# Hybrid decoder trunk: activations stationary, 512 weight columns streaming, in gates, branch products, GLU, w_out and down projection

## The chip, the cores and the metric

The kernel runs on one core of a Trainium2 chip. The metric is the device time of one execution in microseconds (us); the runs below give it for the kernel before. A profile is one execution taken by the hardware profiler; its span runs from the first to the last instruction. TensorE multiplies (PE in the rows, PEld its weight loads), VectorE is DVE, ScalarE ACT, GpSimd POOL, SyncE SP.

## The reference

One layer for 256 tokens of 2048 features, in float32:

```python
hn = rmsnorm(h, norm_mix_w)
proj = hn @ w_in          # u, q, k, v, r, a_lr, dq, dk, dv and the 3 x 2048 gates
y_a = s5_branch(u, ...)   # state space, gelu, @ w_glu, val * sigmoid(gate)
y_b = gla_branch(...)     # linear attention, 4 heads, norm * silu(r), @ gla_w_br
y_c = diff_attn_branch(...)          # 4 heads, norm, @ diff_w_br
g = sigmoid(gates)
merged = g[0] * y_a + g[1] * y_b + g[2] * y_c
h = h + merged @ w_out
h = h + conv_gated_mlp(rmsnorm(h, norm_ffn_w), w_up, conv_w, conv_b, w_down)
out = rmsnorm(h, norm_final_w)
```

## The kernel before

All weights come as 4504 blocks of 128x128 in the order of use, eight blocks (a half chunk, 512 KB) per load. `load` issues the load on SP's queue; `split` rounds it on ScalarE to fp32r (`wh`) and takes the remainder on VectorE (`wl`), three half chunks ahead of their use. Activations are kept the same way, as slots of 512 columns: 256 tokens of the high part, then 256 of the low part, features on the partitions (`hlx`, `hlm`, `hlz`). A product with a weight is high x high + low x high + high x low.

`run` emits the matmuls of a job (one output tile). In kind "a" the weight block is stationary and the activations stream, so that outputs have features on the partitions: a bank of 512 columns holds high and low sums side by side, and `full` adds the two halves (a ScalarE copy, a VectorE add). In kind "b", used for v and dv, the activations are stationary and two weight blocks stream, for each of two token halves; two banks are held and nothing is left to add:

```python
self.mm(bank, wh[:, c:c + P], x, st, False, True)                   # "a", 512 columns
self.mm(bank[:, 0:T], wl[:, c:c + P], x[:, 0:T], False, en, True)   # "a", 256 columns
self.mm(bank, xh, wh[:, c:c + 2 * P], st, False, True)              # "b", 256 columns each
self.mm(bank, xl, wh[:, c:c + 2 * P], False, False, True)
self.mm(bank, xh, wl[:, c:c + 2 * P], False, en, True)
```

The order is written out by hand. After each half chunk `tick` steps every open generator once: evictions (`evs`), attention (`bgs`), and the S5 branch (`s5`) as far as an estimate of VectorE's and ScalarE's load allows. A generator of the last jobs of a stage (`hot`) is urgent: a tick steps it up to 40 times, so that all its instructions are emitted at once. `need` inserts ticks until an input is marked done. Every engine's queue runs in order of emission.

Stages in order: u (8 tiles), the low-rank gate, linear attention (k, q, v, r for 4 heads), differential attention (dq, dk, dv), 16 tiles each of gate B with its branch product and gate C with its own, 7 tiles of gate A (`NA`), GLU with the other gates (S5's result in `hlz` must be done), w_out, FFN up (43 value and 43 gate tiles) and down in two parts. From the end of u until S5 is done three of the eight PSUM banks serve these jobs; the others belong to S5 and the attention heads. The sums of squares of the two later norms (`add_ss`) are squares on ScalarE, adds on GpSimd and a product with a matrix of ones.

Of the kernel before, what the change touches and what calls it, by code (L numbers as in the profile page):

```python
# [34 lines left out]
H_LR = NU * KD // HB  # L35

# [16 lines left out]
class Slots:  # L53
    def __init__(self, aps, slow=False):
        self.aps, self.slow, self.late = aps, slow, []
        self.free = list(range(len(aps)))
        self.back = {}

    def take(self, n):
        if len(self.free) < n:  # L60
            return None
        got, self.free = self.free[:n], self.free[n:]
        return got


def grab(pool, n=1):
    while True:
        got = pool.take(n)
        if got is not None:
            return [(pool, i, pool.aps[i]) for i in got]  # L70
        yield None
# [14 lines left out]
def give(pool, *slots):  # L86
    for _, _, ap in slots:
        pool.free.append(len(pool.aps))
        pool.aps.append(ap)


class Builder:
    SLACK = 1300

    def __init__(self, ctx, tc, wpk, xT, cst, smask, wg, dtab, bpk, cpk, cup, dpk, out):
        self.tc, self.nc = tc, tc.nc
        self.wpk, self.xT, self.cst_d = wpk, xT, cst
# [27 lines left out]
        self.pool = Slots([ar[:, S_END + i * T:S_END + (i + 1) * T] for i in range(N_POOL)])  # L125
        o = S_END + N_POOL * T
        self.evp = Slots([ar[:, o + i * T:o + (i + 1) * T] for i in range(N_EVP)])
        o += N_EVP * T
        self.rp = Slots([ar[:, o + i * T:o + (i + 1) * T] for i in range(N_RES)])
# [192 lines left out]
    def pair(self, a, b, cut):  # L322
        n = len(a[0])
        self.run([a[:2] + ("a", a[2]), b[:2] + ("a", b[2])],
                 [(t, i) for r in (range(cut), range(cut, n)) for t in range(2) for i in r])

    def run(self, tiles, order, hot=()):
        ps = [None] * len(tiles)
        seen = set()
        for t, i in order:  # L330
            xs, evac, kind, keys = tiles[t]
            nb = len(xs)
            per = 2 if kind == "b" else 1
            if ps[t] is None:
                n = 0
                while len(self.g.free) < per:
# [5 lines left out]
                ps[t] = [(self.g, e, self.g.aps[e]) for e in self.g.take(per)]  # L342
# [518 lines left out]
    def ev_v(self, name, h):  # L861
        def gen(ps):
            for t in range(2):
                (s,) = yield from grab(self.pool)
                self.act(s[2], ps[t][2][:, 0:T], AF.Copy)
# [99 lines left out]
    def head_out(self, ob, h, nw, base, rname):  # L965
# [6 lines left out]
        for i in range(2):  # L972
            self.act(S[i][2], ob[2][:, i * T:(i + 1) * T], AF.Square, accum_out=q[:, 20 + i:21 + i])
        if rname:
            for d in range(2):
                yield from self.wait((rname, h, d))
            rr = [self.proj[rname, h, d] for d in range(2)]
            for d in range(2):
                self.act(rr[d][2], rr[d][2], AF.Silu)
        yield from self.rstd(q[:, 20:22], 1.0 / T, q[:, 22:24], self.tiny[:, 0:2], True)  # L980
        for i in range(2):
            self.act(S[i][2], ob[2][:, i * T:(i + 1) * T], AF.Copy, scale=q[:, 22 + i:23 + i])
        drop(ob)
        yield None
# [8 lines left out]
        if rname:  # L993
            for d in range(2):
                self.stt(S[d][2], src[d], nw[:, d:d + 1], rr[d][2], ALU.mult, ALU.mult)
            drop(b, *rr)
            yield None
            for d in range(2):
                self.hilo(dst[d], S[d][2])
            yield None  # L1000
            for d in range(2):
                self.lopart(dst[d], S[d][2])
        else:
            for d in range(2):
                self.hilo(dst[d], src[d], scale=nw[:, d:d + 1])
            yield None
            for d in range(2):
                self.lopart(dst[d], src[d], scale=nw[:, d:d + 1])
            drop(b)
# [5 lines left out]
    def diff_body(self):  # L1015
# [68 lines left out]
        give(self.pool, dt, *S)  # L1084

# [1 line left out]
    def ev_sig(self, name, j, pool):  # L1087
        def gen(ps):
            s = yield from self.full(ps[0])
            yield None  # L1090
            (o,) = yield from grab(pool)
            self.act(o[2], s[2], AF.Sigmoid)
            drop(s)
            self.proj[name, j] = o
            self.done.add((name, j))
        return gen

    def ev_yb(self, j):
        def gen(ps):
            s = yield from self.full(ps[0])  # L1100
            yield from self.wait(("sB", j))
            g = self.proj["sB", j]
            self.tt(g[2], s[2], g[2], ALU.mult)
            drop(s)
            self.proj["m", j] = g
# [385 lines left out]
```

## Time and profile before

| | us |
|---|---|
| device time, median of 3 runs | 1699.87 (1692.81 to 1701.56) |
| the profiled execution, span | 1698.8 |
| TensorE busy in it | 1671.6 (98%) |
| VectorE, ScalarE, GpSimd busy | 1156.9, 975.8, 149.8 |
| granted TensorE clock, mean | 0.992 |

The profiled execution's own time is known as its span; it lies 1.1 us below the median. Busy time of TensorE is a union of listed durations, which overlap their successors: how fast it works is read from the distance between starts.

### The profile page before, as it was taken

The numbers are of one execution on the slowest core, as the hardware profiler recorded it, in microseconds if no ns is written. First come the engines' busy times: TensorE is split into PE (matmuls) and PEld (weight loads), VectorE is DVE, ScalarE is ACT, GpSimd is POOL, SyncE is SP. The second block draws the span as 40 slices with busy tenths as digits, with TensorE's granted clock in tenths as the row PEclk, the third lists the DMA queues.
The fourth block names the chain that finished last, engine by engine and source line by source line (L and its number), as shares of the span: only waits on it lengthen the run. The fifth ranks groups of instructions, "written<-read, shape, count | busy, mean of one in ns | idle before, by whom it ended". The sixth has DMA issues, their size and how long they took to land.

```text
span 1698.8 us, 27107 instructions
## 1 busy us (share of the span) xinstructions
PE 1671.6 (98%) x10352; PEld 1459.3 (86%) x10352; DVE 1156.9 (68%) x1923; ACT 975.8 (57%) x1570; POOL 149.8 (9%) x153
## 2 busy tenths in 40 slices
PE   8899999999999999999999999999999999999996
PEld 7688889999888888888888888888888888888885
DVE  7877667667877677566656777777644677777544
ACT  6557766666566566555555655555544455555553
POOL 1500000000000111000014200000011000000222
PEclk9899999999999999999999999999999999999998
DMA  7567454554656656665555555555555555555552
GB/s 258 167 192 183 144 167 159 167 160 156 211 176 206 204 177 200 199 236 186 186 186 187 186 186 186 186 186 186 186 187 186 185 187 187 186 187 184 189 185 98
DMA packets 111298, 312.97 MB, mean 184 GB/s; under 512 B 27840, under 2 KB 38464, under 8 KB 111040
## 3 DMA queue, kind: packets, MB, share of 16 engines
q1 hardware_dynamic: 109760, 309.54, 56.6%
q8 instruction: 81, 1.33, 0.3%
q10 hardware_dynamic: 1216, 1.18, 0.2%
q0 software_dynamic: 192, 0.52, 0.1%
q14 instruction: 49, 0.40, 0.1%
HBM read 304.64 MB, written 4.19 MB: 182 GB/s over the span
## 4 chain that ended last, share of the span: by engine, by line
PE 96%; DVE 2%; ACT 1%; DMA 1%; issue 0%; DVEq 0%; SPq 0%; ACTq 0%
PE bank L150 95%; PE bank L154 1%; DVE hlx L171 1%; DVE wl L164 0%; DVE ar L164 0%; DMA ar<-in_xT_dram 0%; DMA raw<-in_wpk_dram 0%; ACT ar L158 0%; ACT wh L158 0%; ACT L158 0%; DVEq L1486 0%; ACT hlm L158 0%; DVE ar L171 0%; DVE wh L164 0%; SPq L387 0%
## 5 line engine op out<-in xcount | busy, mean ns | idle before, releaser
L164 DVE TENSOR_TENSOR wl<-raw,wh 128x1024 fp32r<-128x1024 f32 (+1 forms) x564 | 692.0, 1229 | 490.1 <-ACT wh L158 487.1
L150 PE MATMUL bank<-hlx,wh 128*128 128x512 f32 x2656 | 947.6, 398 | 0.0
L158 ACT ACTIVATE wh<-raw 128x1024 fp32r<-128x1024 f32 (+1 forms) x564 | 594.3, 1056 | 604.9 <-issue 319.5
L150 PE MATMUL bank<-hlx,wl 128*128 128x256 f32 x2656 | 748.5, 282 | 0.0
L150 PEld LDWEIGHTS bank<-hlx,wh 128*128 128x128 f32 x2656 | 499.1, 188 | 122.4 <-issue 3.8
L150 PEld LDWEIGHTS bank<-hlx,wl 128*128 128x128 f32 x2656 | 498.9, 188 | 0.2
L150 PE MATMUL bank<-hlm,wh 128*128 128x512 f32 x1152 | 413.3, 398 | 2.6 <-ACT wh L158 2.6
L150 PE MATMUL bank<-hlm,wl 128*128 128x256 f32 x1152 | 326.4, 283 | 1.0 <-DVE wl L164 1.0
L150 PEld LDWEIGHTS bank<-hlm,wh 128*128 128x128 f32 x1152 | 217.9, 189 | 55.7 <-ACT wh L158 3.5
L167 POOL TENSOR_TENSOR ar<-ar 128x256 f32<-128x256 f32 (+2 forms) x127 | 141.8, 1128 | 1218.2 <-ACT ar L158 744.3
L150 PEld LDWEIGHTS bank<-hlm,wl 128*128 128x128 f32 x1152 | 217.8, 189 | 2.0 <-DVE wl L164 1.9
L158 ACT ACTIVATE ar<-bank 128x256 f32<-128x256 f32 (+4 forms) x424 | 152.4, 380 | 28.5 <-PE bank L150 26.7
L150 PE MATMUL bank<-hlz,wh 128*128 128x512 f32 x432 | 154.4, 396 | 0.0
L164 DVE TENSOR_TENSOR ar<-ar 128x256 f32<-128x256 f32 (+5 forms) x360 | 139.6, 392 | 9.2 <-ACT ar L158 1.5
L164 DVE TENSOR_TENSOR ar<-bank,ar 128x256 f32<-128x256 f32 x286 | 118.8, 417 | 12.0 <-ACT ar L158 9.3
L150 PE MATMUL bank<-hlz,wl 128*128 128x256 f32 x432 | 121.8, 282 | 0.0
L158 ACT ACTIVATE ar<-ar 128x256 f32<-128x256 f32 (+3 forms) x209 | 83.9, 413 | 25.6 <-DVE ar L164 21.3
L150 PEld LDWEIGHTS bank<-hlz,wh 128*128 128x128 f32 x432 | 81.2, 188 | 19.6
L150 PE MATMUL bank<-wh,hlx 128*128 128x256 f32 x512 | 90.8, 281 | 0.0
L171 DVE SCALAR_TENSOR_TENSOR ar<-ar,cst 128x256 f32<-128x256 f32 x173 | 83.3, 482 | 5.7 <-ACT ar L158 2.7
L150 PEld LDWEIGHTS bank<-hlz,wl 128*128 128x128 f32 x432 | 81.1, 188 | 0.0
L150 PEld LDWEIGHTS bank<-wh,hlx 128*128 128x128 f32 x512 | 77.7, 188 | 1.9 <-issue 1.4
(81 smaller groups left out, 684.7 us busy)
## 6 DMA issues: line engine op xcount, KB each, us to landing
raw<-in_wpk_dram SPq DMA_DIRECT2D x561, 512.0 KB, 3.5
ar<-in_xT_dram SPq DMA_DIRECT2D x4, 512.0 KB, 7.8
ar<-in_xT_dram SPq DMA_DIRECT2D x1, 2048.0 KB, 8.3
raw<-in_wpk_dram SPq DMA_DIRECT2D x8, 128.0 KB, 5.2
uscr<-ar SPq DMA_DIRECT2D x8, 128.0 KB, 3.5
ar<-in_cpk_dram SPq DMA_DIRECT2D x8, 128.0 KB, 3.1
ar<-uscr SPq DMA_DIRECT2D x8, 128.0 KB, 6.5
zscr<-ar SPq DMA_DIRECT2D x32, 32.0 KB, 3.3
```

What stands on the lines that cost most here:

```text
L150: return self.nc.tensor.matmul(out, lhsT, rhs, start=start, stop=stop)
L154: return self.nc.tensor.transpose(out, in_, self.ident)
L158: return self.nc.scalar.activation(out, in_, func, **kw)
L164: return self.nc.vector.tensor_tensor(out=out, in0=a, in1=b, op=op)
L167: return self.nc.gpsimd.tensor_tensor(out=out, in0=a, in1=b, op=op)
L171: return self.nc.vector.scalar_tensor_tensor(out=out, in0=a, scalar=s, in1=b, op0=op0, op1=op1)
```

## The change

The gates, both branch products, GLU, w_out and the down projection become kind "w": the activations of 128 tokens are stationary, four weight blocks (512 columns) stream into a full bank, six products for four blocks, and the output has tokens on the partitions. A job now covers four former tiles. r becomes kind "b" with Silu on the eviction.

Evictions work on 512 columns straight from the bank, in pairs of neighbouring `pool` slots (`take_wide`). The merged values and h after w_out have tokens on the partitions, while w_out and the up projection need features there: `flip` transposes four tiles on TensorE (eight transposes) and splits them. The sums of squares are taken along the rows with `accum_out`; 1/rms is broadcast for the up projection by a product of ones with a diagonal matrix, and the final norm scales rows. x is loaded a second time in rows (`xN`) instead of columns; the final norm's weights come as an array of 128 equal rows (`wfb`, 1 MB). `NA` is one chunk of four tiles. In GLU the gate comes before the value. The paired first tiles of w_out and up are now two chunks and four tiles, with a cut at 12. The banks and slots of the attention are handed over when its heads are done.

```diff
-            per = 2 if kind == "b" else 1
+            per = dict(a=1, t=1, b=2, w=4)[kind]
...
+            elif kind == "w":
+                n = slice(c, c + 4 * P)
+                for k in range(2):
+                    bank = ps[t][k][2]
+                    self.mm(bank, x[:, k * P:(k + 1) * P], wh[:, n], st, False, True)
+                    self.mm(bank, x[:, T + k * P:T + (k + 1) * P], wh[:, n], False, False, True)
+                for k in range(2):
+                    self.mm(ps[t][k][2], x[:, k * P:(k + 1) * P], wl[:, n], False, en, True)
...
+    def ev_yb(self, c):
         def gen(ps):
+            yield from self.wait(("sB", c))
+            g = self.proj["sB", c]
+            for t in range(2):
+                self.tt(g[t].ap, ps[t][2], g[t].ap, ALU.mult)
+                drop(ps[t])
+            self.proj["m", c] = g
...
+    def flip(self, rows, dst, scale=None):
+        b = yield from grab(self.g, 2)
+        for j in range(4):
+            for t in range(2):
+                self.tr(b[j // 2][2][:, (j % 2) * T + t * P:(j % 2) * T + (t + 1) * P], rows[t][:, j * P:(j + 1) * P])
+        yield None
...
+        for j in range(4):
+            self.hilo(dst[j], src[j], scale=sc[j])
+        yield None
+        for j in range(4):
+            self.lopart(dst[j], src[j], scale=sc[j])
+        drop(*b)
+
+    def ev_val(self, c):
         def gen(ps):
+            yield from self.wait(("gate", c))
+            g, m = self.proj["gate", c], self.proj["m", c]
+            for t in range(2):
+                self.tt(g[t].ap, ps[t][2], g[t].ap, ALU.mult)
+                drop(ps[t])
             yield SOFT
+            for t in range(2):
+                self.tt(m[t].ap, m[t].ap, g[t].ap, ALU.add)
+                drop(*g[t].parts)
+            yield None
+            yield from self.flip([m[t].ap for t in range(2)], [self.slot(self.hlm, 4 * c + j) for j in range(4)])
...
+    def ev_out(self, c):
         def gen(ps):
+            for t in range(2):
+                self.tt(self.hrow(t, c), ps[t][2], self.xrow(t, c), ALU.add)
+                drop(ps[t])
+            yield None
+            yield from self.flip([self.hrow(t, c) for t in range(2)],
...
+            q = self.small
+            yield from self.add_ss(c, q[:, 0:8])
+            self.done.add(("ss", c))
+            if c < 3:
+                return
...
+            yield from self.row_rstd(q[:, 0:8], q[:, 8:10], q[:, 10:12], q[:, 12:14])
+            self.rr, dg = yield from grab(self.pool, 2)
+            for t in range(2):
+                self.ts(dg[2][:, t * P:(t + 1) * P], self.ident, q[:, 8 + t:9 + t], ALU.mult)
+            yield None
+            (b,) = yield from grab(self.mm_)
+            self.mm(b[2][:, 0:T], self.ones, dg[2], True, True)
+            yield None
+            self.act(self.rr[2], b[2][:, 0:T], AF.Copy)
...
-            for d in range(2):
-                self.job(X, self.ev_sum("r", h, d))
+            self.job(X, self.ev_v("r", h, AF.Silu), kind="b")
...
+        for c in range(4):
+            self.job(X, self.ev_sig("sB", c), kind="w")
+            self.job(OG, self.ev_yb(c), kind="w", keys=[("o", k) for k in range(8)])
+        for c in range(4):
+            self.job(X, self.ev_sig("sC", c), kind="w")
+            self.job(OD, self.ev_yc(c), kind="w", keys=[("o", 8 + k) for k in range(8)])
+        for c in range(NA):
+            self.job(X, self.ev_sig("sA", c), kind="w")
         kz = [("z", k) for k in range(8)]
+        for c in range(4):
+            if c >= NA:
+                self.job(X, self.ev_sig("sA", c), kind="w")
+            self.job(Z, self.ev_gate(c), kind="w", keys=kz, hot=c == 3)
+            self.job(Z, self.ev_val(c), kind="w", keys=kz, hot=c == 3)
...
+        self.group([(MG, self.ev_out(c), kmg) for c in range(2)], 12, "w")
+        for c in range(2, 4):
+            self.job(MG, self.ev_out(c), kind="w", keys=kmg, hot=c == 3)
...
                 if f == 0:
-                    self.pair(*up, 14)
+                    first = up
+                elif f == 1:
+                    self.group(first + up, 12)
...
+                if f == 1:
+                    nc.sync.dma_start(self.ar[:, 0:D_MODEL], self.wfb_d)
...
+            for c in range(4):
+                self.job(slots[:nf], ev(c), kind="w", keys=ka, hot=part == 1 and c == 3)
...
+        for t in range(2):
+            h = self.ar[:, KD * T + t * D_MODEL:KD * T + (t + 1) * D_MODEL]
+            self.stt(h[:, n:], h[:, n:], r[t], self.xrow(0, 3), ALU.mult, ALU.mult)
+            (nc.sync, nc.scalar)[t].dma_start(self.out[t][:, n:], h[:, n:])
+            if t == 0:
+                self.ts(h[:, 0:n], h[:, 0:n], r[t], ALU.mult)
+                nc.sync.dma_start(self.out[t][:, 0:n], h[:, 0:n])
             else:
+                for i in range(3):
+                    v = h[:, i * 512:(i + 1) * 512]
+                    self.act(v, v, AF.Copy, scale=r[t])
+                    nc.scalar.dma_start(self.out[t][:, i * 512:(i + 1) * 512], v)
```

## Rows read from the trace of the kernel before

**Rows 1.** the page: busy time of TensorE with its share; the chain that ended last

```profile
PE 1671.6 (98%) x10352; PEld 1459.3 (86%) x10352; DVE 1156.9 (68%) x1923; ACT 975.8 (57%) x1570; POOL 149.8 (9%) x153
...
PE 96%; DVE 2%; ACT 1%; DMA 1%; issue 0%; DVEq 0%; SPq 0%; ACTq 0%
```

**Rows 2.** busy time by stretch, us (instructions): PE, PEld, DVE, ACT, POOL, PEclk, DMA, GB/s

```profile
954.00:1203.00 249.00, 249.00 (x1410) 216.77 (x1409) 190.65 (x305) 146.41 (x222) 2.83 (x3) 1.00 0.56 186
```

**Rows 3.** instructions by line and form: count, busy us, mean ns; the weight split

```profile
L164 DVE TENSOR_TENSOR wl<-raw,wh 128x1024 fp32r<-128x1024 f32 x560 | 689.3, 1232 | 489.5 <-ACT wh L158 486.5 <-PE bank L150 2.4
...
L158 ACT ACTIVATE wh<-raw 128x1024 fp32r<-128x1024 f32 x560 | 591.8, 1059 | 604.3 <-issue 319.5 <-PE bank L150 264.9 <-ACT ar L158 6.4
```

**Rows 4.** timeline of TensorE in GLU: start us, us listed, instruction

```profile
823.64 0.28 PE L150 MATMUL bank<-hlz,wl 128*128 128x256 f32 x1
...
823.76 0.40 PE L150 MATMUL bank<-hlz,wh 128*128 128x512 f32 x1
```

**Rows 5.** the same timeline in two v jobs: undisturbed one, and another

```profile
83.51 0.39 PE L150 MATMUL bank<-wh,hlx 128*128 128x256 f32 x2
...
94.39 0.39 PE L150 MATMUL bank<-hlx,wh 128*128 128x512 f32 x1
...
166.21 0.40 PE L150 MATMUL bank<-wh,hlx 128*128 128x256 f32 x2
...
168.33 0.40 PE L150 MATMUL bank<-wh,hlx 128*128 128x256 f32 x2
```

**Rows 6.** the same timeline at the second norm: ones products (fp32)

```profile
959.08 1.02 PE L150 MATMUL bank<-ar,cst 128*128 128x256 f32 x4
...
960.17 0.28 PE L150 MATMUL bank<-hlx,wl 128*128 128x256 f32 x1
```

**Rows 7.** the same timeline at eight transposes of the linear attention

```profile
145.07 1.03 PE L154 MATMUL bank<-cst,ar 128*128 128x128 f32 x8
...
146.18 0.28 PE L150 MATMUL bank<-hlx,wl 128*128 128x256 f32 x1
```

**Rows 8.** instructions by line and form: the nearest to the added steps

```profile
L164 DVE TENSOR_TENSOR ar<-ar,misc 128x512 f32<-128x512 f32 x32 | 20.7, 688 | 0.6
...
L158 ACT ACTIVATE ar<-bank 128x512 f32<-128x512 f32 x24 | 13.3, 592 | 0.2 <-PE bank L154 0.2
...
L158 ACT ACTIVATE hlm<-bank,misc 128x256 fp32r<-128x256 f32 x8 | 3.3, 472 | 0.0
...
L158 ACT ACT_TABLE_LOAD x51 | 65.4, 1283 | 1.6 <-PEq L1477 0.7
...
L171 DVE SCALAR_TENSOR_TENSOR misc<-misc 128x2 f32<-128x2 f32 x24 | 3.8, 157 | 0.6
...
L176 DVE TENSOR_SCALAR ar<-ar,misc 128x128 f32<-128x128 f32 x4 | 1.1, 280 | 0.0
```

**Rows 9.** busy time by stretch around TensorE's pause before the linear attention

```profile
56.00:58.00 2.00, 0.41 (x3) 0.09 (x1) 2.00 (x3) 2.00 (x5) 2.00 (x3) 1.00 0.00 0
...
58.00:60.00 2.00, 0.00 (x0) 0.00 (x0) 2.00 (x4) 1.85 (x2) 2.00 (x3) 0.58 0.00 0
...
64.00:66.00 2.00, 1.51 (x6) 1.42 (x7) 2.00 (x6) 0.17 (x1) 0.00 (x0) 0.50 0.61 240
...
68.00:70.00 2.00, 2.00 (x14) 1.52 (x16) 0.00 (x0) 0.21 (x1) 0.09 (x1) 0.86 1.04 348
```

**Rows 10.** DMA issues: KB each, median us to landing; the second load of x

```profile
ar<-in_xT_dram SPq DMA_DIRECT2D x1, 2048.0 KB, 8.3
```

**Rows 11.** timeline of the tail: last down product, last scaling

```profile
1683.86 0.28 PE L150 MATMUL bank<-hlz,wl 128*128 128x256 f32 x1
...
1693.93 0.47 DVE L171 SCALAR_TENSOR_TENSOR ar<-ar,cst 128x256 f32<-128x256 f32 x1
```

**Rows 12.** hlz's instructions (ns min/median/max, first, last start us); VectorE's timeline

```profile
L150 PE MATMUL bank<-hlz,wh x432: 392/397/399, 721.6 to 1683.6; 128*128 128x512 f32 x144
...
721.18 1.19 DVE L164 TENSOR_TENSOR hlz<-ar,hlz 128x256 fp32r<-128x256 f32 x2
```

More of the change, by code (lines that the diff above doesn't have):

```diff
@@ L70, in grab, with __init__, grabw @@
             return [(pool, i, pool.aps[i]) for i in got]
+        yield None
+class Wide:
+    def __init__(self, pool, pair):
+        self.parts = [(pool, i, pool.aps[i]) for i in pair]
+        o = pool.offs[pair[0]]
+        self.ap = pool.arena[:, o:o + 2 * T]
+def grabw(pool):
+    while True:
+        pair = pool.take_wide()
+        if pair is not None:
+            return Wide(pool, pair)
         yield None
@@ L341, in run @@
                     self.stalls.append(("bank", n, self.h))
[L342 removed]
+                ps[t] = [(self.g, e, self.g.aps[e]) for e in self.g.take(nbank)]
             if keys is not None:
@@ L1084, in diff_body @@
         give(self.pool, dt, *S)
-    def ev_sig(self, name, j, pool):
-        def gen(ps):
-            s = yield from self.full(ps[0])
-            yield None
[L1091 to L1095, printed above, removed]
+        while any(("o", k) not in self.done for k in range(16)):
+            yield None
+        give(self.pool, *self.ho)
+        while len(self.mm_.free) < 2 or len(self.ops_.free) < 1:
+            yield None
@@ new lines, in diff_body, with ops_bank, ev_sig @@
+        give(self.g, self.ops_bank(), (None, None, self.mm_.aps[self.mm_.free.pop()]))
+    def ops_bank(self):
+        self.ops_.free = []
+        return (None, None, self.ops_.aps[0])
+    def ev_sig(self, name, c):
+        def gen(ps):
+            out = []
+            for t in range(2):
+                o = yield from grabw(self.pool)
+                self.act(o.ap, ps[t][2], AF.Sigmoid)
+                drop(ps[t])
+                out.append(o)
+            self.proj[name, c] = out
+            self.done.add((name, c))
+        return gen
@@ L1121, in ev_val @@
-    def ev_val(self, j):
-        def gen(ps):
-            s = yield from self.full(ps[0])
-            self.proj["val", j] = s
-            self.done.add(("val", j))
-        return gen
-    def ev_gate(self, j):
-        def gen(ps):
-            s = yield from self.full(ps[0])
+            yield from self.wait(("sA", c))
+            a = self.proj["sA", c]
+            out = []
+            for t in range(2):
+                o = yield from grabw(self.pool)
+                self.act(o.ap, ps[t][2], AF.Sigmoid)
+                drop(ps[t])
+                out.append(o)
@@ L1327, in build @@
                     self.job(X, up[1][1], hot=last)
+                if f == 1:
+                    nc.sync.dma_start(self.ar[:, 0:D_MODEL], self.wfb_d)
             ka = [("act", f) for f in range(f0, f0 + nf)]
-            dn = [(slots[:nf], (self.ev_downA if part == 0 else self.ev_downB)(j), ka) for j in range(KD)]
-            self.pair(dn[0], dn[1], nf - 2)
-            for j in range(2, KD):
-                self.job(slots[:nf], dn[j][1], hot=part == 1 and j >= KD - 2)
+            ev = self.ev_downA if part == 0 else self.ev_downB
```

358 lines of the change are left out of this document (171 added, 187 removed).

## The prediction

> **What bounds the kernel now.** Read the busy table of the page first, then the chain of work that ended last: TensorE is busy for 1671.6 of 1698.8 us and carries 96% of the chain [rows 1]. The stretches tell the same without the start and the tail: in 954 to 1203 us TensorE is busy all 249 us at a granted clock of 1.00, while VectorE and ScalarE stand at 77% and 59% [rows 2]. So between 70 and 1684 us only two things can move the end: the spacing of the matmuls, and a new wait that stops TensorE. Taking work off VectorE and ScalarE gains nothing by itself: their largest item, splitting each 1024 columns of weights (1.06 us, then 1.23 us), fits in the 2.83 us that TensorE takes for the same half chunk and stays as it is [rows 3].
>
> The spacing needs start-to-start times, because the listed durations overlap. In that stretch 1410 matmuls take 249 us, 353.2 ns for two, and two are one 128x128 block of weights (512 columns with the high part, then 256 with the low). In the timeline the narrow one holds its place for 0.12 us [rows 4], so the wide one takes 0.233. The arithmetic is 768 columns, 320 ns at 2.4 GHz: a tenth of the time is not columns.
>
> The kernel already has the other orientation, activations stationary and weights streaming, in the v and dv jobs (kind "b", three products of 256 columns for each token half, six for two blocks, the same 768 columns for each block). Its timeline shows two spacings. One undisturbed job of 96 products runs from 83.51 to 94.39 us: 113.3 ns each, 340 ns for a block. In another job 18 products take 166.21 to 168.33 us: 117.8 ns, 353 ns for a block, no better than kind "a" [rows 5]. Nothing else in those rows differs, so this bistable spacing is the main unknown.
>
> **The change part by part.** *Rate.* The gates (768 blocks), branch products (256), GLU (256), w_out (256) and the down projection (688) become kind "w": 2224 blocks, four at a time, six products of 512 columns for four blocks, again 768 columns for each. The r job (128 blocks) becomes kind "b". 1376 up-projection blocks, u, q, k, dq and dk stay kind "a". No row shows a stationary activation with 512 weight columns. The nearest rows bound it:
> - the fp32 ones product streams 256 columns twice in each record; four records take 960.17 - 959.08 - 0.233 = 0.857 us, 214 ns for 512 streamed columns, 321 ns for a block [rows 4, 6];
> - the "b" rows, doubled, give 226.7 or 235.6 ns, that is 340 or 353 ns for a block [rows 5];
> - the same shape with swapped roles (512 columns, kind "a") gives 0.233 us, 350 ns [rows 2, 4].
>
> I take 340: the operand roles are those of "b", and its undisturbed job holds that spacing from end to end. That saves 353.2 - 340 = 13.2 ns on 2352 blocks, 31.0 us. The bounds are 0 and 75 us.
>
> The Trainium skill ("TensorE: Matmul & The Clock Gate", section "Back-to-back issue gap") gives the warm gap as columns / 2.4 plus 2.5 ns, 215.8 ns for 512 columns. By that estimate a block takes 324 ns, and the sum below would give 1649 us instead of 1688. The trace agrees with it for the fp32 records (214 ns) and not for the 512-column products of kind "a" (233 ns) [rows 4, 6].
>
> *Flips.* Merged values and h now have tokens on the partitions, and the next product needs features there: eight flips of eight transposes. Eight such transposes and the product behind them take 145.07 to 146.18 us, 0.88 us without that product's 0.233 [rows 4, 7]. They are TensorE's own work: 8 x 0.88 = +7.0 us. Of the ones products behind the two norms, one of four records goes and one of two comes: -0.4 us.
>
> *A wait at the flip of the last GLU chunk.* Urgent generators (the last chunk of a stage, `hot`) are emitted whole in one tick, so the transposes stand in TensorE's queue right behind the first half chunk of w_out, although VectorE must first do two products and two adds of 512 columns. VectorE is free for them 2.3 us into that half (1.06 + 1.23 [rows 3]), needs 4 x 0.69 = 2.8 us [rows 8] and is done at 5.1; TensorE arrives at 2.7. The wait is +2.4 us. Queued behind it is all of w_out. The other three flips of a stage come one tick later than their adds, 2.7 us, and are covered.
>
> *A wait at the second norm.* The last w_out chunk is urgent as well. Its two adds end at 3.7 us, TensorE arrives at 2.83: +0.9. After 0.88 us of transposes, the broadcast of 1/rms (a ones product with a diagonal) is the next thing in TensorE's queue, and it needs four evictions on ScalarE (4 x 0.47), two squares of 512 columns (2 x 0.59), three sums of two columns on VectorE (0.16 each), the rsqrt with its table load (1.28, and a small step like the others), three more small steps (0.16 each) and two scalings (0.28 each) [rows 8]. That adds to 6.1 us with nothing between for TensorE; all of the up projection is queued behind it. The table load may run beside the small sums, so I take 6.0. The trace shows what such a pause costs besides: when TensorE went idle in 56 to 58 us the granted clock was at half (1.2 GHz) by 58 to 60, and after work resumed in 64 to 66 it came back to full (2.4 GHz) only in 68 to 70 [rows 9]: some 4 us at half rate, 2 us lost. Together +8.9. Bounds: 0, because before the same ones product stood one half chunk later and TensorE met it without a gap (959.08 [rows 6]); and 12 if nothing overlaps.
>
> *Banks.* Until the attention heads are done, early in the branch products, only three PSUM banks serve these jobs, and a "w" or "b" job holds two. The next job's second bank must be drained first: one 592 ns eviction on ScalarE or 688 ns on VectorE [rows 8] against 4 x 113 ns of cover, so 0.2 to 0.5 us at about three boundaries, less at the four v to r boundaries (three products of cover, a shorter eviction). I take +2.0, bounds 0 and 5. A column of 512 in `pool` needs two adjacent free slots; a late one would lengthen the same waits.
>
> *DMAs.* The later load of x has the same size. The final norm's weights add 1 MB on SP's queue ahead of the weight loads. They stand three to four half chunks ahead (8 to 11 us), and a 2 MB load landed in about 8 us before [rows 10], so 4 us of delay is hidden: 0. Without that cover it would cost those 4.
>
> *Tail.* Before, from the last down product (1683.86) to the end of the span it is 14.9 us; the last scaling ends at 1694.40, 4.4 us before the end [rows 11]. After: add (0.7, the first bank is ready early), square (0.6), three sums (0.5), table load and rsqrt (1.4), three steps (0.5), scalings (0.7 + 1.0 + 0.7), three ScalarE scalings with their stores (about 3, by 0.59 for each [rows 8] and as much for its store), and the same 4.4 us of landing: 13.5, about 13.9 with the hand-overs. I take -1, bounds -4 and +3.
>
> Sum: 1698.8 - 31.0 + 7.0 - 0.4 + 2.4 + 8.9 + 2.0 - 1.0 = 1686.7 us of span. The median of the runs is 1699.9, 1.1 above this span: 1688.
>
> Everything but the rate adds 18.9 us. So the change breaks even at 353.2 - 18.9 / 2.352 = 345.2 ns for a block, 230 ns for a product of 512 columns. Half a per cent (8.5 us) is about what a measurement of this kernel can tell from no change.
>
> **The rivals.**
> 1. *Overhead belongs to the instruction, not to the column.* Kind "b" spends 113.3 - 106.7 = 6.6 ns beyond its columns [rows 5]; 512 columns would take 220, a block 330, saving 54.6 us: 1664. For: fewer instructions (six for eight). Against: in kind "a" the wide product's excess (20 ns) is larger than the narrow one's (13) [rows 4].
> 2. *Only the columns count* (fp32 row, 321 ns for a block [rows 6]): 75.7 us saved, 1643. Against: the 512-column products of kind "a" [rows 4]. The Trainium skill's rule ("TensorE: Matmul & The Clock Gate", section "Back-to-back issue gap") is this case a few us later, 1649.
> 3. *Slower: the spacing of kind "a" stays.* If 512 columns take 0.233 us whatever the roles, a block takes 350, the saving is 7.5 us, and the flips and waits (18.9) decide: 1711. With the slow "b" spacing (353) it is 1718. It decides from 230 ns for a product upward. For: the shape is the same; against: the undisturbed "b" job.
> 4. *In between*, the two "b" spacings alternate: 346.7 for a block, 15.3 us saved, 1703.
> 5. *The S5 branch is late.* GLU's inputs were done at 722.4 us and first read at 721.6 [rows 12]; now only 64 instead of 112 blocks of gates stand ahead (17 us less), while the last input is read 28 instead of 7 blocks into GLU (7 us more). S5 must be some 10 us earlier. Less eviction work on ScalarE and VectorE speaks for it; if it fails, up to +10 us on any case: 1698 on the forecast.
>
> **How the numbers follow.** Chances: forecast 0.32 (1680 to 1695), rival 1 0.20, rival 2 0.08, rival 3 0.24, rival 4 0.11, rival 5 on the forecast 0.05. The time is that of the forecast, 1688. The range leaves out rival 2 and the upper end of rival 3 with the slow spacing: 1660 to 1716. Faster by over 0.5% (under 1691.4): rivals 1 and 2 and most of the forecast, 0.54. Slower (over 1708.4): most of rival 3 and some of rivals 4 and 5, 0.23. Within: 0.23.
>
> **What would show it.** Rate: the timeline of the down projection, start to start of 512-column products (226.7 forecast; 220, 214, 233 the rivals), at a granted clock of 1.00. Flips: eight transposes in 0.9 us. The norm: a gap of about 6 us on TensorE just behind the first half chunk of the up projection, with the ones product released by VectorE and half clock behind it; a gap of about 2.4 us near the start of w_out. S5: no gap at the start of GLU. The prediction is wrong if the spacing is not near 227, or if the gaps are missing or larger than 12 us.

## The result and the profile after

The change makes the kernel slower: 1715.5 us (median; 1709.5 to 1716.8) against 1700.8 us for the kernel before on the same chip, ratio 1.0083 with a 95% interval of 1.006 to 1.0105. Forecast were 1688 us; the time that was measured is that of rival 3 (1711), a few us above. The profiled execution has a span of 1710.9 us, 12.1 more than that of before.

The page, its busy times: TensorE 98% as before [rows 1], VectorE and ScalarE a little lower, GpSimd a third. TensorE still sets the time.

```profile
PE 1673.2 (98%) x9426; PEld 1411.6 (83%) x9426; DVE 1106.3 (65%) x1759; ACT 913.4 (53%) x1345; POOL 55.0 (3%) x58
```

Where the 12.1 us come from is read from the start of each stage (first product in either trace):

| first product of | before, us | after, us | behind by |
|---|---|---|---|
| gates | 394.02 | 394.69 | 0.7 |
| w_out | 862.98 | 868.44 | 5.5 |
| up projection, first part | 953.44 | 963.19 | 9.8 |
| down, first part | 1203.02 | 1221.77 | 18.8 |
| up, second part | 1327.39 | 1344.97 | 17.6 |
| down, second part | 1564.83 | 1579.43 | 14.6 |
| last product | 1683.86 | 1696.80 | 12.9 |
| end of the span | 1698.8 | 1710.9 | 12.1 |

Kind "w" gains almost nothing: 688 blocks of the down projection win 1.2 + 1.7 us, 4 ns for each. By the end of the first part of the up projection the change is 18.8 us behind: up to there the flips and waits cost more than the rate has won.

The timeline of TensorE in the first down projection of after, the first row of `hlm` and the first of `hlz` (start us, us listed, instruction):

```profile
1221.77 1.10 PE L190 MATMUL bank<-wh,hlm 128*128 128x512 f32 x4
...
1244.17 1.09 PE L190 MATMUL bank<-wh,hlz 128*128 128x512 f32 x4
```

96 products lie between the two, 22.40 us: 233.3 ns for each, 350.0 for a block. In the start times 494 of the 555 groups of six products take 1.400 us to the ns or so; it is one spacing, held nearly everywhere, at a granted clock of 1.00. That is what the 512-column product of kind "a" takes [rows 2, 4].

An ordinary flip, the GLU flip of the last chunk, and the second norm in the same timeline; in brackets the idle time before the row and what ended it:

```profile
736.54 0.63 PE L190 MATMUL bank<-wl,hlx 128*128 128x512 f32 x2
737.01 1.04 PE L194 MATMUL bank<-cst,ar 128*128 128x128 f32 x8
737.80 0.94 PE L190 MATMUL bank<-wh,hlx 128*128 128x512 f32 x3
...
870.77 0.63 PE L190 MATMUL bank<-wl,hlm 128*128 128x512 f32 x2
872.34 0.33 PE L194 MATMUL bank<-cst,ar 128*128 128x128 f32 x1 [0.94 <-DVE ar L204]
872.94 0.98 PE L194 MATMUL bank<-cst,ar 128*128 128x128 f32 x7 [0.27 <-DVE ar L204]
873.68 1.18 PE L190 MATMUL bank<-wh,hlm 128*128 128x512 f32 x4
...
966.01 0.27 PE L194 MATMUL bank<-cst,ar 128*128 128x128 f32 x1
966.50 0.98 PE L194 MATMUL bank<-cst,ar 128*128 128x128 f32 x7 [0.22 <-DVE ar L204]
972.77 1.22 PE L190 MATMUL bank<-ar,cst 128*128 128x256 f32 x2 [5.29 <-DVE ar L216]
973.43 0.99 PE L190 MATMUL bank<-hlx,wh 128*128 128x512 f32 x1
```

The flip takes 737.80 - 737.01 = 0.79 us. At the last GLU chunk the next product could have started at 870.77 + 2 x 0.233 = 871.24 and starts at 873.68: 2.44 us, 1.6 without the flip. The norm stops TensorE for 5.3 us, and the clock goes with it. Busy time by stretch (PE, PEld, DVE, ACT, POOL, then the granted clock):

```profile
970.00:972.00 2.00, 0.00 (x0) 0.00 (x0) 0.64 (x4) 1.59 (x3) 0.00 (x0) 0.89 0.00 0
972.00:974.00 2.00, 1.23 (x3) 1.05 (x4) 0.65 (x4) 0.00 (x0) 0.00 (x0) 0.50 0.00 0
976.00:978.00 2.00, 2.00 (x7) 1.68 (x7) 0.62 (x1) 0.00 (x0) 0.00 (x0) 0.50 0.23 45
978.00:980.00 2.00, 2.00 (x12) 1.72 (x11) 0.15 (x1) 1.06 (x1) 0.00 (x0) 0.90 0.58 217
```

Level 0.50 (1.2 GHz) lasts over 4 us into the work, 7 matmuls in 2 us where 12 and more run at full clock.

Two more gaps stand where the gates begin, at bank changes. TensorE, and what ScalarE and VectorE did in that time:

```profile
394.69 0.71 PE L190 MATMUL bank<-wh,hlx 128*128 128x512 f32 x2
397.15 0.73 PE L190 MATMUL bank<-wh,hlx 128*128 128x512 f32 x2 [1.74 <-ACT ar L198]
...
432.71 0.63 PE L190 MATMUL bank<-wh,hlx 128*128 128x512 f32 x2
435.21 0.86 PE L190 MATMUL bank<-wh,hlx 128*128 128x512 f32 x2 [1.88 <-DVE ar L204]
```

```profile
395.33 2.04 ACT L198 ACTIVATE ar<-bank 64x128 f32<-64x128 f32 x7
```

```profile
432.03 1.22 DVE L204 TENSOR_TENSOR wl<-raw,wh 128x1024 fp32r<-128x1024 f32 x1
433.16 0.87 DVE L211 SCALAR_TENSOR_TENSOR hlm<-bank,misc,hlm 128x256 fp32r<-128x256 f32 x2
433.95 0.21 DVE L204 TENSOR_TENSOR ar<-ar 128x64 f32<-128x64 f32 x1
434.20 0.36 DVE L204 TENSOR_TENSOR ar<-ar,misc 128x64 f32<-128x64 f32 x2
434.48 1.28 DVE L204 TENSOR_TENSOR ar<-bank,ar 128x512 f32<-128x512 f32 x2
```

The eviction that frees the bank (434.48) stands in VectorE's queue behind the split and the attention's steps; in ScalarE's queue it is the same. After the second gap the clock is at 0.50 again in 436 to 438 us. That is not so in every run: with a pause of 1.8 to 1.9 us at the same place the clock stayed at 1.00 in e1, e2 and e4, and in e10, after a longer one:

```profile
438.60 0.73 PE L191 MATMUL bank<-wh,hlx 128*128 128x512 f32 x2 [2.65 <-DVE ar L205]
```

```profile
438.00:440.00 2.00, 1.40 (x6) 1.00 0.59 215
```

### The profile page after: what moved, and what is told of

Same layout as the page of the kernel before. It is cut to its first block, busy times and chain, and to the rows that moved or that the text cites. A ratio compares the mean times of both kernels' runs of the same rounds, so it can differ in the third digit from the quotient of the medians.

```text
span 1710.9 us, 24705 instructions
## 1 busy us (share of the span) xinstructions
PE 1673.2 (98%) x9426; PEld 1411.6 (83%) x9426; DVE 1106.3 (65%) x1759; ACT 913.4 (53%) x1345; POOL 55.0 (3%) x58
## 4 chain that ended last, share of the span: by engine, by line
PE 74%; DVE 1%; ACT 1%; issue 0%; ACTq 0%; DVEq 0%
PE bank L190 74%; DVE ar L204 1%; DVE wl L204 1%; PE bank L194 1%; ACT ar L198 0%; ACT wh L198 0%; ACT L198 0%; DVE misc L211 0%; DVE ar L211 0%; ACT hlx L198 0%; DVEq L1588 0%; DVE hlm L211 0%; ACTq L1446 0%; ACT misc L198 0%; ACTq L1438 0%
## 5 line engine op out<-in xcount | busy, mean ns | idle before, releaser
L190 PE MATMUL bank<-hlx,wh 128*128 128x512 f32 x1760 | 625.3, 397 | 0.0
L190 PE MATMUL bank<-hlx,wl 128*128 128x256 f32 x1760 | 495.9, 282 | 0.0
L190 PEld LDWEIGHTS bank<-hlx,wh 128*128 128x128 f32 x1760 | 332.1, 189 | 80.2 <-issue 1.9
L190 PE MATMUL bank<-wh,hlx 128*128 128x256 f32 (+1 forms) x1536 | 350.0, 340 | 4.6 <-ACT ar L198 2.7
L190 PEld LDWEIGHTS bank<-hlx,wl 128*128 128x128 f32 x1760 | 331.3, 188 | 0.3
L190 PEld LDWEIGHTS bank<-wh,hlx 128*128 128x128 f32 x1536 | 260.4, 189 | 42.4 <-ACT ar L198 3.3
L190 PE MATMUL bank<-wh,hlm 128*128 128x512 f32 x1024 | 281.4, 396 | 0.0
L190 PEld LDWEIGHTS bank<-wh,hlm 128*128 128x128 f32 x1024 | 191.1, 188 | 46.7 <-ACT ar L198 0.4
L190 PE MATMUL bank<-wl,hlx 128*128 128x256 f32 (+1 forms) x768 | 228.3, 338 | 0.0
L190 PE MATMUL bank<-wl,hlm 128*128 128x512 f32 x512 | 160.8, 395 | 0.0
L190 PEld LDWEIGHTS bank<-wl,hlx 128*128 128x128 f32 x768 | 144.8, 189 | 17.6
L204 DVE TENSOR_TENSOR ar<-ar 128x256 f32<-128x256 f32 (+5 forms) x306 | 117.8, 389 | 7.1 <-ACT ar L198 1.0
```

The lines of the kernel that those rows point to most:

```text
L190: return self.nc.tensor.matmul(out, lhsT, rhs, start=start, stop=stop)
L204: return self.nc.vector.tensor_tensor(out=out, in0=a, in1=b, op=op)
```

## The experiments

Medians in us; ratios to the kernel before on the same chip, with their intervals. "Alike" and "apart" are explained below. The runs e3, e5 and e7 are not in the table: they add products of their own behind the kernel's, and only the spacing of these is read, from one execution each.

| run | edit | median | ratio |
|---|---|---|---|
| after | | 1715.5 | 1.0083 (1.0060 to 1.0105) |
| e1 | pauses ahead of flips and norm | 1706.4 | 1.0040 (1.0028 to 1.0052) |
| e4 | each flip twice | 1719.4 | 1.0121 (1.0091 to 1.0152) |
| e2 | kind "w" in 256 columns | 1704.4 | 1.0028 (1.0010 to 1.0047) |
| e8 | weight tiles alike | 1694.8 | 0.9976 (0.9961 to 0.9991) |
| e9 | before, weight tiles alike | 1694.9 | 0.9959 (0.9944 to 0.9974) |
| e10 | e1 and e8 | 1688.6 | 0.9932 (0.9916 to 0.9949) |
| e6 | e1 and e2 | 1693.1 | 0.9961 (0.9949 to 0.9973) |
| e11 | e6, weight tiles alike | 1718.9 | 1.0110 (1.0095 to 1.0125) |
| e12 | e10, evictions ahead of attention steps | 1691.1 | 0.9942 (0.9926 to 0.9959) |

### The waits and the flips

e1 lets the urgent generators pause (`HALT` ends a generator's turn in a tick): a half chunk of matmuls is issued ahead of the last flips, three ahead of the norm's ones product.

```diff
...
-                n -= self.step(self.evs, g) is not SOFT
+                r = self.step(self.evs, g)
+                n = 0 if r is HALT else n - (r is not SOFT)
...
-            yield None
+            for _ in range(3):
+                yield HALT
             (b,) = yield from grab(self.mm_)
             self.mm(b[2][:, 0:T], self.ones, dg[2], True, True)
```

> The changed kernel, but an urgent generator now pauses for one half chunk ahead of its transposes and for three ahead of the ones product of the second norm, so that TensorE has other products in between. Theory (the two waits cost what their gaps show: about 1.6 us at the flip behind GLU, 0.5 us and 5.3 us at the norm, and some 2.2 us of half clock behind it): the gaps near 872 and 966 to 973 us go, and the time falls by about 10 us against the changed kernel, to some 1.002 to 1.004 of the kernel before. Rival (the gaps are only the place where TensorE waits for something else that comes due later, such as the weight split): the gaps move behind the pauses and the time falls by under 3 us.

1706.4 us, 9 less than after. The gaps at the flip and the norm are gone, and with them the stretch at half clock; the flip of the last w_out chunk now stands between matmuls:

```profile
967.21 0.28 PE L191 MATMUL bank<-hlx,wl 128*128 128x256 f32 x1
967.33 1.04 PE L195 MATMUL bank<-cst,ar 128*128 128x128 f32 x8
968.12 0.48 PE L191 MATMUL bank<-hlx,wh 128*128 128x512 f32 x1
```

So the two waits were real and priced about right, and they were no necessary part of the change. The half clock at 436 us is missing here as well, though its gap stays (1.9 us); whether it comes moves a time by 1.5 us, and the pauses have no part in that.

e4 issues the eight transposes of each flip twice:

```diff
-        for j in range(4):
+        for j in [*range(4)] * 2:
             for t in range(2):
                 self.tr(b[j // 2][2]...
```

> The changed kernel with the eight transposes of each flip issued twice. Theory (the flips are TensorE's own time, 0.88 us each): 7 us more than the changed kernel, about 1.0125 of the kernel before. Rival (transposes fit beside other work): no difference above 2 us.

Medians differ by 3.9 us, the two profiled spans by 10.0 (1720.9 and 1710.9). The times show that flips cost some us, and no better than that. The trace has the price: sixteen transposes hold TensorE for 1.66 us (926.66 to 928.32 us, to the start of the next product), eight for 0.79, so 0.87 more for each flip and 7.0 us in all, as expected.

### The spacing: width, operands or addresses

e2 streams the same weights in two products of 256 columns each, except in the first and last product of a sum:

```diff
...
-                    self.mm(bank, x[:, T + k * P:T + (k + 1) * P], wh[:, n], False, False, True)
...
+                    for o in (0, T):
+                        self.mm(bank[:, o:o + T], x[:, T + k * P:T + (k + 1) * P], wh[:, c + o:c + o + T], False, False, True)
```

> The changed kernel, but each product of kind w streams 256 columns twice in place of 512 once (only the first and the last product of a bank's sum keep 512). Theory (the roles of the operands decide nothing, the width does: 256 columns have a fast spacing of 113.3 ns and a slow one of 117.8, 512 columns have 233.3 alone): the products show 113.3 or 117.8 ns, a block takes 340 or 353 ns in place of 350, and the time moves by -22 us (all fast) to +7 us (all slow) against the changed kernel. Rival (a 10 per cent excess per column whatever the width): 116.7 ns everywhere, the same time within 3 us. Rival (each product carries a fixed overhead of some 20 ns): 127 ns, a block at 380 ns, some 65 us longer.

11 us faster than after, with twice the products: the down projection runs at 113.3 ns for 256 columns, the "b" value of [rows 5]; in GLU and w_out a part runs at 117.8. So the operand roles were not what was wrong, and there is no fixed price for each instruction (rival 1). 512 columns take more than twice 256.

e3 asks on a free TensorE what 512 columns can do: 800 products from `hlx` and `hlm` behind the last down job of the kernel before, in stretches of one shape.

> The kernel before with eight stretches of products added behind the last down product, which go to no output: 64 of 512 columns; 128 of 256; 64 of 512 with the same stationary operand each time; 64 of 512 and 128 of 256 with a stationary operand of 32 columns; 512 and 256 in turn; 128 of 128; and 512, 256, 256 in turn. Theory (the excess belongs to streaming fp32r columns): 233 ns for 512 columns in all three stretches, however short the weight load, 113 to 118 for 256, and 353 for the pair in turn. Rival (the weight load behind each product costs the excess): with 32 stationary columns, whose load is a quarter as long, 512 columns take 216 ns and 256 take 109. Rival (a fixed overhead per product): 128 columns take 53 plus 20 ns or, bound by the weight load, 109.

Mean spacing in the start times: 226.7 ns for 512 columns, 120.0 for 256, 226.7 for 512 with one stationary tile kept, 231.7 and 113.3 with 32 stationary columns, 176.7 for 512 and 256 in turn (353.4 a pair), 111.7 for 128, 156.8 for 512, 256 and 256 in turn. Both the theory (233 for 512 columns in every stretch) and the rival of the weight load (216 with 32 stationary columns) missed. Here 512 columns do run at the forecast's 226.7, and 256 at 120.0, slower than in the kernel. So it is neither the width nor the weight load alone; something turns the order round.

e5 takes the pattern of kind "w" apart on the same free TensorE: its banks, its order of stationary tiles, its order of moving tiles, its moving tiles themselves.

> The kernel before, with 480 extra 512-column products behind its last down job, in eight stretches of 60 on a free TensorE; the page's time means nothing. Stretches 1 and 8: one bank, stationary and moving tile step on with each product (the pattern that ran at 226.7 ns). Each of the others brings in one part of what kind w does: 2 the order of its two banks, 3 its order of stationary tiles, 4 its order of moving tiles, 5 all three, 6 all three with the weight tiles themselves as moving operand, 7 the weight tiles as moving operand alone. Theory: 226.7 ns in 1 and 8, and one part of the pattern that brings 233.3, seen in its own stretch and again in 5 and 6. Rival: the spacing is a state that is taken up by chance when a stretch begins, not bound to the pattern: then 226.7 and 233.3 fall among the eight without order, and the change's 233.3 in nearly all of its products is not explained by the pattern alone.

The five stretches that stream from `hlm` run at 226.7 to 226.8 ns whatever the order, the two that stream from weight tiles at 233.2 and 233.3, the last one from `hlm` at 226.7. The timeline has it as blocks: 300 products from 1684.29 to 1752.32 us are 226.8 ns each, and six from the weight tiles 1.40 us:

```profile
1752.32 1.09 PE L150 MATMUL bank<-whb,hlx 128*128 128x512 f32 x4
...
1753.72 1.09 PE L150 MATMUL bank<-whb,hlx 128*128 128x512 f32 x4
```

By the allocation `hlx` and `hlm` begin at a multiple of 128 bytes of their partition, and every weight tile 64 bytes past one, because the small tile `misc` ahead of them is 2240 bytes long. e7 moves single operands by 64 or 32 bytes.

> The kernel before with 720 extra products behind its last down job, twelve stretches of 60; only their spacing is read, the page's time means nothing. In e5 the same 512 columns took 226.7 ns streamed from hlm and 233.3 ns streamed from the weight tiles wh and wl. By the allocation hlm and hlx begin at a multiple of 128 bytes of their partition, wh and wl 64 bytes past one. Stretches: 1 and 9 both operands at a multiple of 128 bytes; 2 the moving operand 64 bytes on; 3 the moving operand 32 bytes on; 4 the stationary operand 64 bytes on; 5 both 64 bytes on; 6 weight tiles moving as they lie; 7 weight tiles moving, read from 64 bytes on, so from a multiple of 128; 8 weight tiles stationary; 10 to 12 products of 512 and 256 columns in turn, with both at a multiple, the stationary one 64 bytes on, the moving one 64 bytes on. Theory (address): 233.3 in 2, 5 and 6, 226.7 in 1, 4, 7 and 9; 3 is open. Rival (region of the memory or what else uses it): 2 stays at 226.7 and 7 stays at 233.3. Rival (state taken up at a stretch's start, whatever the operand): no order among them.

| stretch | moving at | stationary at | ns a product |
|---|---|---|---|
| 1, 9 | 0 | 0 | 227.0, 226.7 |
| 2 | 64 | 0 | 228.9 |
| 3 | 32 | 0 | 233.2 |
| 4 | 0 | 64 | 233.4 |
| 5 | 64 | 64 | 226.9 |
| 6 | weight tile as it lies, 64 and 0 by turns | 0 | 233.1 |
| 7 | weight tile read from 64 on, 0 and 64 by turns | 0 | 226.9 |
| 8 | 0 | weight tile, 64 | 229.0 |
| 10 to 12 | 512 and 256 in turn: moving/stationary 0/0, 0/64, 64/0 | | 353, 353, 353 a pair |

(Bytes past a multiple of 128.) In stretches 6 and 7 every second product begins 496 columns (1984 bytes) further on, which is 64 bytes past a multiple of 128. So each of the two has both offsets, and not one as its expectation says. A few products at the start of a stretch differ; without them the means are three values, 226.7 (stretches 1, 5, 7, 9), 228.9 (2, 8) and 233.3 (3, 4, 6). The timeline inside stretches 4 and 5, where only the moving operand goes on by 64 bytes:

```profile
1725.83 13.46 PE L150 MATMUL bank<-hlm,hlx 128*128 128x512 f32 x57
...
1740.29 12.40 PE L150 MATMUL bank<-hlm,hlx 128*128 128x512 f32 x54
```

Less the 0.4 us that one product is listed with, that is 233 ns for each of 56 and 226 for each of 53. And at the boundary of stretches 6 and 7, where every product of 7 begins 64 bytes further on in the same tiles:

```profile
1752.98 2.02 PE L150 MATMUL bank<-whb,hlx 128*128 128x512 f32 x8
...
1764.17 2.03 PE L150 MATMUL bank<-whb,hlx 128*128 128x512 f32 x8
...
1766.97 1.98 PE L150 MATMUL bank<-whb,hlx 128*128 128x512 f32 x8
...
1777.86 1.98 PE L150 MATMUL bank<-whb,hlx 128*128 128x512 f32 x8
```

48 products take 11.19 us before and 10.89 us behind it: 233.1 and 226.9 ns. Where a stretch has one offset throughout (1 to 5, 8, 9), it counts where the two operands stand to each other: at the same place within 128 bytes ("alike") a product takes 226.7 to 227.0, otherwise ("apart") 228.9 to 233.4. The expectation, that the moving operand alone decides, was wrong in stretches 4 and 5, and too high in 2. For the pair of kind "a" it makes no difference in these stretches (10 to 12).

That is not the whole rule. Stretches 4 and 8 have the same two places within 128 bytes and take 233.4 and 229.0; stretches 6 and 7 have the same two offsets by turns and take 233.1 and 226.9. And with 32 stationary columns (e3) operands that stood alike took 231.7 and 113.3. By the allocation, counted within 512 bytes, the moving operand begins 64 bytes above the stationary one in stretches 2 and 8 (228.9 ns) and 64 bytes below it in 4 (233.3), as in kind "w" of the change (233.3). So the direction may count too; no run tests it.

### The spacing in the kernel

e8 is after with one number changed, so that all weight tiles begin at a multiple of 128 bytes; e9 is the kernel before with the same edit; e10 adds e1's pauses to e8.

```diff
-        self.misc = sb.tile([P, 560], F32, name="misc")
+        self.misc = sb.tile([P, 576], F32, name="misc")
```

> The change with one number changed: the small tile ahead of the weight tiles is 64 bytes longer, so that raw, wh and wl begin at a multiple of 128 bytes, as hlx, hlm and hlz do. Theory (e7: 512 columns take 226.7 to 226.9 ns when both operands stand alike within 128 bytes, 228.9 to 233.4 when not): the 512-column products of kind w go from 233.3 to 226.7 ns, 3330 products x 6.6 = -22 us: 1715.5 - 22 = 1693, ratio to before about 0.996. Kind a (512 and 256 columns in turn, 353 to 355 ns for a block in each stretch of e7) stays. Rival, that e7's stretches show something that long sums with weights from the transfers don't have: 1715, no change.

> The kernel before with the same 64 bytes. Theory: its products are nearly all of kind a, whose pair of 512 and 256 columns took 353 to 355 ns in e7 whichever operand was moved on, and only its v and dv jobs (512 blocks of 256-column products) can gain, up to 13 ns a block, 7 us: 1694 to 1702, ratio 0.996 to 1.001. Rival, that the offset of its weight tiles held back all its products: 4700 blocks x 13 ns = 61 us, 1640.

> The change with the pauses of e1 and the 64 bytes of e8. Theory, two independent prices: 1706.4 - 22 = 1684, ratio to before about 0.990, close to what the prediction gave for the rate, with no waits at the norm. Rival: 1706, as e1.

e8 gains 20.7 us on after, as expected. The same two rows of the down projection:

```profile
1210.53 1.08 PE L190 MATMUL bank<-wh,hlm 128*128 128x512 f32 x4
...
1232.30 1.07 PE L190 MATMUL bank<-wh,hlz 128*128 128x512 f32 x4
```

96 products in 21.77 us, 226.8 ns, 340 for a block: the forecast's rate, from 64 bytes. 476 of the 555 groups of six take 1.360 us. The "b" jobs went the other way. In the v job of [rows 5] the rows of e8 and after:

```profile
83.79 0.40 PE L190 MATMUL bank<-wh,hlx 128*128 128x256 f32 x2
...
93.50 0.40 PE L190 MATMUL bank<-wh,hlx 128*128 128x256 f32 x2
```

```profile
84.00 0.39 PE L190 MATMUL bank<-wh,hlx 128*128 128x256 f32 x2
...
92.84 0.39 PE L190 MATMUL bank<-wh,hlx 128*128 128x256 f32 x2
```

81 products in 9.71 us with the operands alike, 119.9 ns; 78 in 8.84 us apart, 113.3 ns. So 512 columns want their operands alike and 256 apart.

Kind "a" stays in e8. Its second part of the up projection, by its matmul count, runs as before's first part [rows 2], 353 ns for a block:

```profile
1350.00:1550.00 200.00, 200.00 (x1135) 1.00 0.56 187
```

e9 is 5.6 us faster than before, inside the expected range but not for the expected reason: its "b" jobs became slower (120 ns), and the gain is in kind "a", which now runs part of the way at 346.7 ns for a block instead of 353.3. That the 64 bytes choose this is not shown: with the same 64 bytes kind "a" stays at 353 in e8. (The expectation counts 512 blocks of v and dv; there are 256.) The same stretch by its matmul count, in before and in e9:

```profile
700.00:900.00 200.00, 200.00 (x1134) 1.00 0.60 200
```

```profile
700.00:900.00 200.00, 200.00 (x1155) 1.00 0.61 203
```

With the same offset before (e9, 1694.9) and after (e8, 1694.8) are equal: the change's rate pays for its flips and waits and no more. With the pauses (e10, 1688.6) the change is worth about 6 us, with six runs of e9 between 1689.1 and 1696.5. For e10 1684 was expected: by the medians the pauses gain 6.2 us on e8, not 9.1; the two profiled spans differ by 9.9 (1695.8 and 1685.8).

e6 joins e1 and e2; e11 is e6 with the 64 bytes.

> The change with the pauses of e1 (waits gone) and the 256-column products of e2 (narrower spacing) together. Theory, two independent prices: 1715.5 - 9 - 11 = 1695, ratio to before about 0.997. Rival, that both gains are partly the same (the narrower products in e2 won because the gaps moved): 1702 to 1705, ratio 1.001 to 1.003.

> e6 (pauses, 256-column products in kind w) with the 64 bytes of e8. In e8 the 256-column products of kind b went from 113.3 (or 117.8) to 120.0 ns when the operands stood alike, while the 512-column ones went from 233.3 to 226.7. Theory, that the two widths want opposite offsets: the 256-column products of kind w go to 120 ns too, 360 ns a block against about 345 in e6, on 2220 blocks of which most are 256 wide: +25 us or more, 1715 to 1725. Rival, that alike is always better: below 1693.

1693.1 us and 1718.9, both as expected. In e11 24 products of 256 columns take 2.87 us, 120 ns, in e2 (operands apart) 2.72 us, 113.3 ns:

```profile
1229.76 1.12 PE L191 MATMUL bank<-wh,hlm 128*128 128x256 f32 x8
...
1232.63 1.12 PE L191 MATMUL bank<-wh,hlm 128*128 128x256 f32 x8
```

```profile
1230.39 1.07 PE L190 MATMUL bank<-wh,hlm 128*128 128x256 f32 x8
...
1233.11 1.07 PE L190 MATMUL bank<-wh,hlm 128*128 128x256 f32 x8
```

The same 64 bytes that gain e8 20.7 us cost e6 25.8: the two widths want opposite offsets.

### The banks

e12 is e10 with the evictions of a bank issued ahead of the attention's steps while fewer than two banks are left.

```diff
...
+            early = en and kind in ("b", "w") and t not in hot and len(self.g.free) < 2
+            if early:
+                self.evs.append(evac(ps[t]))
             if per and self.b % HB == 0:
                 self.wt.pop(h)
                 self.tick()
-            if en:
+            if en and not early:
```

> e10 with one change of order: where fewer than two banks are left, the evictions of a b or w job are issued ahead of the attention steps of the same tick, not behind them. In the change the bank of the first gate job waited 1.7 us at 397 us and 1.9 us at 435 us (and 2 us more at half clock); in e10 1.6 and 2.7 us. Theory, that the bank's eviction stood in ScalarE's and VectorE's queues behind the attention's steps: the waits go, -4 us, 1684.5, no gap over 1 us between 390 and 450 us. Rival, that the eviction itself with the weights' split ahead of it takes that long: 1688.5, gaps stay.

The gaps at the gates go (1.6 and 2.7 us in e10, none and 0.4 here), and the time still rises by 2.6 us: neither theory. The waits of TensorE in e10 and in e12 (us in total, times, longest):

```profile
PE bank L191 <- DVE ar L205: 2.7, 1, 2.7
PE bank L191 <- ACT ar L199: 2.0, 2, 1.6
```

```profile
PE bank L195 <- ACT ar L199: 4.2, 2, 2.7
PE bank L191 <- ACT hlz L199: 4.0, 1, 4.0
```

The steps that stand behind the evictions now are late themselves: the attention's transposes wait 4.2 us, and GLU waits 4.0 us for S5 (718.81 us), whose last conversion on ScalarE waits for its data:

```profile
718.13 1.17 ACT L199 ACTIVATE hlz<-ar 128x256 fp32r<-128x256 f32 x2 [5.36 <-DMA ar<-zscr]
```

That is rival 5, called up by an edit elsewhere. In after the last input of S5 was done about 1 us ahead of its use.

## Why the prediction was wrong

*Rate: the step that failed.* "The operand roles are those of 'b', and its undisturbed job holds that spacing": 226.7 ns was the doubled price of a 256-column product whose operands stood apart. Doubling a width was the fault, not the roles (e2, e5). The product of 512 columns with operands apart takes 233.3, and the kernel has no other offset. Measured from both profiles: 2224 x (353.2 - 350.0) = 7.1 us gained, and about 1 by the r jobs, where 31.0 were forecast; 23 us of the 24 between the predicted span (1686.7) and the measured one (1710.9); the misses in the other terms nearly cancel. Rival 3 had the number, and in part by luck. [rows 4] showed 512 columns and [rows 5] did not, but kind "w" does not simply keep the spacing of kind "a": in e8 64 bytes take it to 226.8 and leave kind "a" at 353 for a block. That the rate itself exists (e8: 340 for a block) was out of sight of the trace of before.

The Trainium skill ("TensorE: Matmul & The Clock Gate", section "Back-to-back issue gap") gives 215.8 ns for 512 columns by its formula, which it calls the gap of an isolated product. No steady stream of 512-column fp32r products in these runs came below 226.7. The Trainium skill's "SBUF — State Buffer" (section "A bandwidth-pool intuition that's wrong") lists a second, independent read port for weight loads. In e7 the spacing hangs on the places of both operands together (226.7, 228.9, 233.4 and 226.9 in stretches 1, 2, 4 and 5); whether the ports have to do with it is not shown.

*Flips.* Right: 8 x 0.79 = 6.3 us, forecast 7.0.

*The wait at the last GLU chunk.* Right in its place and cause, 1.6 us for 2.4.

*The second norm.* Right: from 966.01 to 973.43 us are 7.4, without flip and ones product 6.1, and the seven blocks from there to 978.27, at half clock, take 4.84 us where 2.47 would do, 2.4 more: 8.5 for 8.9. e1 shows both waits by taking them out.

*Banks.* Mis-sized: 1.7 + 1.9 us of gaps, 1.0 at 94.3 us (`v` to `r`), 1.5 by the half clock: 6.1, forecast 2.0 and at most 5. The sum took the eviction's own 0.6 us; what TensorE waits for is its place in a queue, behind the split and the attention's steps. That the clock fell at the pause of 1.9 us is not the rule: it fell again in e6 (2.3 us), and not in e1, e2, e4, e8 and e10 (1.8 to 2.7 us at the same place); the length of the pause alone does not decide it.

*The rest.* The tail is 14.1 us for 14.9 (forecast -1, measured -0.8). S5 was in time. One gain was not foreseen: kind "a" ran the second part of the up projection at 349 ns for a block in this execution, 3 us less. In all -31.0 + 7.0 - 0.4 + 2.4 + 8.9 + 2.0 - 1.0 = -12.1 became about -8 + 6.3 - 0.4 + 1.6 + 8.5 + 6.1 - 0.8 - 3 = +10.3; the spans say +12.1, so 1.8 us have no row here.

With the forecast's rate (e8, span 1695.8) 9.1 us are still missing from 1686.7. Most of them are the "b" jobs at 360 ns for a block, not 340 to 353 (256 blocks of v and dv by some 15, 128 of r by 20: 6.4 us), and banks at 4.6 us of gaps, 2.6 more than forecast. As the flips and the GLU wait came 1.5 us cheaper than forecast, some 1.6 us stay open.

## What to carry to other kernels

Take the price of a matmul from a row with its own width and its own tiles; neither twice a half-wide product nor the same shape out of other tiles is a bound. Where TensorE sets the time and its spacing is a few per cent above the columns, look at where the two operands begin and try 64 bytes of padding, before and after a change, and measure it: here it was worth more than the change (20.7 us on after, 5.6 on before), and with 256-column products it cost 25.8. And an eviction that frees a bank costs what stands ahead of it in its engine's queue; putting it first makes what was ahead late.

## What the runs showed of the hardware that was not expected

- fp32r products hold one of few spacings, exactly, for hundreds of products: 226.7, 228.9 or 233.3 ns (512 columns), 113.3, 117.8 or 120.0 (256), 346.7, 349.0 or 353.3 for the pair of kind "a".
- The offset of the operands to each other, 64 bytes, chooses among them, and in opposite ways for 512 (alike 226.7, apart 233.3) and 256 columns (alike 120.0, apart 113.3 or 117.8), with 128 stationary columns and the addresses of these kernels. The full rule is open (stretches 4 and 8, 6 and 7 of e7), and why is not shown. What picks 113.3 or 117.8 with operands apart, and 346.7 or 353.3 in kind "a" with operands alike, stays open too: both were seen at the same offset in one execution, and in the traces looked at the change from one to the other came only where the stream of products was interrupted. Weight tiles alike for kind "w" and apart for kind "b" in one kernel were not tried.
- The second part of the up projection in after ran 1148 matmuls in 200 us, the first 1134, with nothing changed in code or tiles. Such a choice moves single executions of one kernel by 3 us and more, so a difference of that size needs many of them.
